# A decoder trunk on one core: the first stage on 2048 columns with unsplit float32 operands, conditioning rows in one piece, gates by themselves

## The chip, the core and the metric

One program runs on one core of a Trainium2 chip. The core has five engines with their own instruction streams: TensorE (PE: matmul, its weight loads shown as PEld), VectorE (DVE), ScalarE (ACT), GpSimd (POOL) and SyncE (SP), which here issues nearly all DMA transfers. Matmul results go to PSUM, eight banks of 512 float32 per partition; everything else lives in SBUF. The metric is the time of one execution on the device in microseconds.

## The reference

Two layers on a sequence of 256 tokens, model width 2048. A conditioning vector c gives six vectors of 2048 per layer (shift, scale and gate of two sub-layers); each comes from a matrix of 2048 x 2048 in `ada_w`. Everything is float32.

```python
mod_all = einsum('bd,lde->lbe', silu(c), ada_w) + ada_b
for i in range(2):
    sh1, sc1, g1, sh2, sc2, g2 = split(mod_all[i], 6)
    h = rms_norm(x, attn_norm_g[i]) * (1.0 + sc1) + sh1
    y = nsa_mixer(h, ...) if i == 0 else diff_mixer(h, ...)
    x = x + g1 * y
    h = rms_norm(x, mlp_norm_g[i]) * (1.0 + sc2) + sh2
    x = x + g2 * (square(relu(h @ w1)) @ w2)
```

The first mixer multiplies h by one matrix and cuts the result: q (2048 columns), kc and vc (512 each, keys and values that are compressed in blocks by two small matrices), ks and vs (512 each, selection branch), kw and vw (512 each, window branch), and 48 gates that weigh the three branches.

## The kernel before

**Layout.** Activations stand transposed: 16 tiles of 128 features (`kt`) by 256 tokens. A float32 operand is mostly split into two parts of a faster matmul type (float32r): ScalarE rounds it to a high part `wH`, VectorE subtracts to get the low part `wL` (`split`, L219), and a product takes three matmuls (`xs_mm`, `ws_mm`, L234 to L248). The normalised h is split in the same way into four activation tiles (`modulate`, L320).

**First stage (L603 to L622).** For each of the 16 `kt` it needs one column of the scale and one of the shift, each a sum over 2048 elements per partition. `ada_tile` (L160) loads such rows in halves of 1024 into `adaraw` (pool `ada`, three buffers) and VectorE multiplies by silu(c) and sums. The scale is computed so for all `kt`; the shift so for six of them; for the ten in `PEK` TensorE takes it (`ada_pe`, L173: `adapw`, a tile of 1 MB in the activation pool, and 16 float32 matmuls). Then the weights `ws` of this `kt` come in two pieces (1024 and 560 columns: kc, vc, vs, gates), are split, h of this `kt` is made, and the products for kc and vc (four PSUM tiles), vs (two) and the gates (one) are accumulated over `kt`.

**After it.** `xs_group` (L253) runs one group of 512 weight columns: four units, each two loads of 512 KB, two splits and 24 matmuls of 512 columns. The groups are ks (`k0_`), kw (`k1_`), vw (`vw_`), then four q groups, each followed by the attention of four heads whose work lies under the next group. In the two k groups each unit also does eight float32 matmuls of the compression (`hidps`, weights `cw1`). `k_block` (L700) norms and rotates the keys; its transposes wait in the list `pend` and are emitted by `pop` in the next group. After each unit `ada_step(rate)` loads rows for the later conditioning vectors, `RA` (1.1) rows per unit in k and vw groups, `RB` (1.0) in q groups; they are halves of 512 KB in the three `ada` buffers, computed on VectorE with a lowered priority.

**Queues.** All these loads are issued by SP in one order. An issue that waits for its buffer holds what stands behind it. Weight tiles `raw` have five buffers, activation tiles eight, four of which hold h. The order of instructions on each engine is set by a scheduler from the program's order, priorities and estimated times.

Of the kernel before, what the change touches and what calls it, by code (L numbers as in the profile page):

```python
# [19 lines left out]
P = 128  # L20
T = 256
# [6 lines left out]
# Points of a pair of groups where the statistics and the first group's results are taken.  # L28
# [7 lines left out]
# Tiles of the adaLN matrices taken per unit of weights, by phase.  # L36
RA, RB, RC = 1.1, 1.0, 1.6
# [5 lines left out]
# Columns of the first shift that the tensor engine takes.  # L43
PEK = [k for k in range(16) if k % 8 not in (2, 5, 7)]
# [14 lines left out]
WS_COLS = 3 * 512 + GATES  # L59
# [18 lines left out]
def emit(ctx, tc, nc, a):  # L78
# [103 lines left out]
    def ada_one(l, vec, kt):  # L182
        e = vec * KT + kt
        ac = acc_tile(l, vec)
        stt(mod[:, l, vec, kt:kt + 1], ac[:, kt, 0:1], bT[:, l, e:e + 1], ac[:, kt, 1:2], ALU.add, ALU.add)
# [32 lines left out]
    # Exact split of float32 into two float32r parts.  # L218
# [222 lines left out]
    # A norm whose first two products run on A*x before the statistics are known: the results are  # L441
    # scaled by rstd afterwards, and two further columns carry the shift through the weights.
# [156 lines left out]

    ps_c = [[mm_tile(f"psc{i}{b}") for b in range(2)] for i in range(2)]  # L600
    ps_v = [sc(f"psv{t}") for t in range(TT)]
    ps_g = sd("psg")
    for kt in range(KT):  # L603
        ada_tile(0, 1, kt)
        if kt in PEK:
            ada_pe(kt)
        else:
            ada_tile(0, 0, kt)
            ada_one(0, 0, kt)
        ada_one(0, 1, kt)  # L610
        stt(Amod[:, 0, 0, kt:kt + 1], mod[:, 0, 1, kt:kt + 1], 1.0, ag[:, 0, kt:kt + 1], ALU.add, ALU.mult)
        H, L = split(load(a["ws"][kt, :, :1024]))
        H2, L2 = split(load(a["ws"][kt, :, 1024:], WS_COLS - 1024), WS_COLS - 1024)
        modulate(h, kt, rstd, Amod[:, 0, 0, kt:kt + 1], mod[:, 0, 0, kt:kt + 1])
        f, la = kt == 0, kt == KT - 1
        for i in range(2):
            for n in range(4):
                ws_mm(ps_c[i][n // 2][:, (n % 2) * T:(n % 2 + 1) * T], h, kt, H, L, i * 512 + n * P, f and n % 2 == 0,
                      la and n % 2 == 1)
        for t in range(TT):  # L620
            xs_mm(ps_v[t], h, kt, t, H2, L2, 0, 512, f, la)
        ws_mm(ps_g[:GATES, :T], h, kt, H2, L2, 512, f, la, m=GATES)  # L622
    kcT = [actp.tile([P, GROUPS, 272], F32, tag="act", name=f"kcT{i}") for i in range(2)]
    for i in range(2):
        V.memset(kcT[i][:, :, 256:272], 0.0)
        for b in range(2):
            act(kcT[i][:, b * 2:b * 2 + 2, 0:T], ps_c[i][b].rearrange("p (g t) -> p g t", g=2))
    for t in range(TT):
        act(Vt[:, t, 0, :], ps_v[t])

    gT = wkp.tile([P, T], F32, tag="PcT", name="gT", bufs=1)
    act(gT[:48, :], ps_g[:48, :T])
    for t in range(TT):
# [399 lines left out]
```

## Time and profile before

| what | value |
|---|---|
| median of 3 runs | 2420.01 us (2419.43 to 2420.33) |
| the profiled execution: its own time, which is its span | 2418.4 us |
| PE busy | 2368.7 us, 98% |
| DVE busy | 1706.2 us, 71% |
| ACT busy | 1179.3 us, 49% |
| moved by DMA | 612.79 MB, mean 253 GB/s |
| first stage: start of the first and the last gate matmul | 31.7 and 157.9 us |
| q groups: start of the first and the last matmul | 266.0 and 420.6 us |
| mean granted TensorE clock | 0.996 |

Busy time is the sum of an engine's instruction spans; matmuls overlap in the pipeline, so their single durations are longer than their spacing. The granted clock is the share of 2.4 GHz at which TensorE was allowed to run; 0.5 is the lower of its two levels, 1.2 GHz. The DMA share is the mean busy share of the 16 DMA engines in a stretch.

### The profile page before, as it was taken

What the parts mean: (1) busy time and instruction counts of PE and PEld (TensorE: products, weight loads), DVE (VectorE), ACT (ScalarE), POOL (GpSimd) and SP (SyncE); (2) the same over time, 40 slices, a digit from 0 to 9 for tenths busy, and PEclk for the clock granted to TensorE, in tenths of its full rate; (3) what the DMA queues carried; (4) which work ended last, traced back from release to release, by engine and by line L of the source; (5) the groups of instructions that cost most, each with busy time, mean ns of one, the idle gap of its engine ahead of it and who ended that gap; (6) DMA issues with size and microseconds to landing.
All of it is one profiled execution on the core that took longest, in us unless ns stands there. A gap on an engine that the chain in (4) does not pass through costs nothing.

```text
span 2418.4 us, 44106 instructions
## 1 busy us (share of the span) xinstructions
PE 2368.7 (98%) x17683; PEld 2233.3 (92%) x17683; DVE 1706.2 (71%) x2670; ACT 1179.3 (49%) x1939; POOL 39.4 (2%) x41
## 2 busy tenths in 40 slices
PE   8889899999999999999999999999999999999999
PEld 6876677999999999999999788799999999999999
DVE  6786898999878888878897766656745445455444
ACT  3233477656434434434546655555643443443443
POOL 0000000000000000000000101100000000000000
PEclk9999999999999999999999999999999999999999
DMA  8988875787888888888986565445555555555554
GB/s 331 351 315 308 301 279 204 285 317 286 339 342 333 327 342 338 333 328 337 335 306 215 200 228 173 162 152 182 181 186 185 184 183 184 188 186 183 184 193 147
DMA packets 168973, 612.79 MB, mean 253 GB/s; under 512 B 18880, under 2 KB 20288, under 8 KB 167488
## 3 DMA queue, kind: packets, MB, share of 16 engines
q1 hardware_dynamic: 167616, 609.06, 68.6%
q8 instruction: 138, 2.26, 0.4%
q10 hardware_dynamic: 1152, 0.92, 0.2%
q14 instruction: 67, 0.55, 0.1%
HBM read 607.81 MB, written 2.10 MB: 252 GB/s over the span
## 4 chain that ended last, share of the span: by engine, by line
PE 88%; DVE 5%; DMA 3%; ACT 2%; issue 1%; POOL 1%; SPq 0%; DVEq 0%; ACTq 0%; POOLq 0%
PE m L248 19%; PE m L247 19%; PE m L246 19%; DVE wL L100 2%; DMA adaraw<-adaT 2%; DVE adaraw L103 1%; PE adps L178 1%; PE dwo L247 1%; PE dwo L246 1%; PE dwo L248 1%; PE m_z L248 1%; PE m_z L246 1%; PE m_z L247 1%; PE dq L239 1%; PE dq L238 1%
## 5 line engine op out<-in xcount | busy, mean ns | idle before, releaser
L100 DVE TENSOR_TENSOR wL<-raw,wH 128x1024 fp32r<-128x1024 f32 x760 | 920.1, 1214 | 568.3 <-ACT wH L97 565.6
L97 ACT ACTIVATE wH<-raw 128x1024 fp32r<-128x1024 f32 x760 | 796.9, 1051 | 999.2 <-PE m L247 615.4
L248 PE MATMUL m<-hd,wL 128*128 128x256 f32 x2048 | 576.6, 282 | 1.0 <-DVE wL L100 1.0
L247 PE MATMUL m<-hd,wH 128*128 128x256 f32 x2048 | 576.7, 282 | 0.0
L246 PE MATMUL m<-hd,wH 128*128 128x256 f32 x2048 | 576.4, 282 | 0.0
L247 PE MATMUL m<-hn,wH 128*128 128x256 f32 x1792 | 504.4, 282 | 0.0
L248 PE MATMUL m<-hn,wL 128*128 128x256 f32 x1792 | 503.7, 281 | 0.0
L246 PE MATMUL m<-hn,wH 128*128 128x256 f32 x1792 | 503.2, 281 | 0.0
L103 DVE SCALAR_TENSOR_TENSOR adaraw<-adaraw,cbc 128x1024 f32<-128x1024 f32 x364 | 438.3, 1220 | 21.7 <-DMA adaraw<-adaT 21.2
L248 PEld LDWEIGHTS m<-hd,wL 128*128 128x128 f32 x2048 | 387.2, 189 | 1.5 <-DVE wL L100 1.4
L247 PEld LDWEIGHTS m<-hd,wH 128*128 128x128 f32 x2048 | 386.7, 189 | 0.0
L246 PEld LDWEIGHTS m<-hd,wH 128*128 128x128 f32 x2048 | 386.2, 189 | 0.1
L246 PEld LDWEIGHTS m<-hn,wH 128*128 128x128 f32 x1792 | 338.5, 189 | 0.2 <-ACT zb L97 0.2
L248 PEld LDWEIGHTS m<-hn,wL 128*128 128x128 f32 x1792 | 338.4, 189 | 0.0
L247 PEld LDWEIGHTS m<-hn,wH 128*128 128x128 f32 x1792 | 337.7, 188 | 0.0
L248 PE MATMUL nwo<-o,wL 128*128 128x256 f32 x256 | 72.9, 285 | 2.6 <-DVE wL L100 2.6
L246 PE MATMUL nwo<-o,wH 128*128 128x256 f32 x256 | 73.4, 287 | 0.3 <-ACT wH L97 0.3
L246 PE MATMUL dwo<-od,wH 128*128 128x256 f32 x256 | 72.8, 284 | 0.0
L247 PE MATMUL nwo<-o,wH 128*128 128x256 f32 x256 | 72.4, 283 | 0.0
L248 PE MATMUL m_z<-z,wL 128*128 128x258 f32 x256 | 70.1, 283 | 2.4 <-DVE wL L100 2.4
L247 PE MATMUL dwo<-od,wH 128*128 128x256 f32 x256 | 72.1, 282 | 0.0
L248 PE MATMUL dwo<-od,wL 128*128 128x256 f32 x256 | 72.0, 281 | 0.0
(312 smaller groups left out, 3399.3 us busy)
## 6 DMA issues: line engine op xcount, KB each, us to landing
raw<-w SPq DMA_DIRECT2D x512, 512.0 KB, 4.5
adaraw<-adaT SPq DMA_DIRECT2D x364, 512.0 KB, 5.7
raw<-di SPq DMA_DIRECT2D x96, 512.0 KB, 3.6
raw<-wi SPq DMA_DIRECT2D x56, 512.0 KB, 6.3
raw<-nwo SPq DMA_DIRECT2D x32, 512.0 KB, 4.7
raw<-dwo SPq DMA_DIRECT2D x32, 512.0 KB, 3.2
adapw<-adaP SPq DMA_DIRECT2D x10, 1024.0 KB, 8.0
raw<-ws SPq DMA_DIRECT2D x16, 512.0 KB, 8.5
```

Of the source, the lines that this page charges most:

```text
L97: return S.activation(out=out, in_=in_, func=func, **kw)
L100: V.tensor_tensor(out=out, in0=in0, in1=in1, op=op)
L103: V.scalar_tensor_tensor(out, in0, scalar, in1, op0=op0, op1=op1, **kw)
L178: TE.matmul(ps[:, :P], r[:, k, :], cs[:, k:k + 1].to_broadcast([P, P]), start=(k == 0), stop=(k == KT - 1))
L238: TE.matmul(ps, xh, H[:, off:off + n], start=first, stop=False)
L239: TE.matmul(ps, xh, L[:, off:off + n], start=False, stop=False)
L246: TE.matmul(ps, H[:, off:off + m], xh, start=first, stop=False)
L247: TE.matmul(ps, H[:, off:off + m], xl, start=False, stop=False)
L248: TE.matmul(ps, L[:, off:off + m], xh, start=False, stop=last)
```

## The change

The first stage takes 2048 columns of weights (kc, vc, vs, vw) instead of 1584, in two tiles of 1024 columns, and multiplies them as they are: `modulate_full` keeps an unsplit h of the `kt` beside the split one, and the matmuls are float32. All eight PSUM tiles of the three pools hold results. Scale and shift are both done on VectorE for every `kt`, each as one instruction over 2048 elements (`ada_row`), from tiles in the activation pool. The gates are computed by `gates()` behind the kw group, from weights of their own. The vw group falls away; `pop` is called in the q groups; `RA` and `RB` become 1.3 and 1.2.

```diff
-RA, RB, RC = 1.1, 1.0, 1.6
+RA, RB, RC = 1.3, 1.2, 1.6
-WS_COLS = 3 * 512 + GATES
+WS_COLS = 4 * 512
-    def ada_pe(kt):
-        ps = sc("adps")
-        r = actp.tile([P, KT, P], F32, tag="act", name="adapw")
-        nc.sync.dma_start(r, a["adaP"][PEK.index(kt)])
-        for k in range(KT):
-            TE.matmul(ps[:, :P], r[:, k, :], cs[:, k:k + 1].to_broadcast([P, P]),
-                      start=(k == 0), stop=(k == KT - 1))
-        ts(mod[:, 0, 0, kt:kt + 1], ps[:, 0:1], bT[:, 0, kt:kt + 1], None, ALU.add)
+    def ada_row(vec, kt):
+        r = actp.tile([P, D], F32, tag="act", name="adarow")
+        nc.sync.dma_start(r.rearrange("p (j d) -> p j d", j=2),
+                          a["adaT"][0, vec * KT + kt].rearrange("j p d -> p j d"))
+        acc = acc_tile(0, vec)[:, kt, 0:1]
+        stt(r, r, 1.0, cbc, ALU.mult, ALU.mult, accum_out=acc)
+        return acc
+    def modulate_full(tiles, kt, rstd, A, sh):
+        t = sm.tile([P, T], F32, tag="nsq", name="nt0", bufs=4)
+        stt(t, xT[:, kt, :], A, rstd, ALU.mult, ALU.mult)
+        full = sm.tile([P, T], F32, tag="pp", name="h32", bufs=4)
+        act(full, t, AF.Identity, bias=sh)
+        H = tiles[kt // 4][:, 0, kt % 4, :T]
+        act(H, full)
+        tt(tiles[kt // 4][:, 1, kt % 4, :T], full, H.bitcast(F32), ALU.subtract)
+        return full
-    ps_v = [sc(f"psv{t}") for t in range(TT)]
-    ps_g = sd("psg")
+    ps_v = [[sc("psv00"), sc("psv01")], [sc("psv10"), sd("psv11")]]
     for kt in range(KT):
...
-        H, L = split(load(a["ws"][kt, :, :1024]))
-        H2, L2 = split(load(a["ws"][kt, :, 1024:], WS_COLS - 1024), WS_COLS - 1024)
-        modulate(h, kt, rstd, Amod[:, 0, 0, kt:kt + 1], mod[:, 0, 0, kt:kt + 1])
+        acc = ada_row(1, kt)
+        stt(Amod[:, 0, 0, kt:kt + 1], acc, b1[:, kt:kt + 1], ag[:, 0, kt:kt + 1], ALU.add, ALU.mult)
+        acc = ada_row(0, kt)
+        tt(mod[:, 0, 0, kt:kt + 1], acc, bT[:, 0, kt:kt + 1], ALU.add)
+        wc = load(a["ws"][kt, :, :1024])
+        wv = load(a["ws"][kt, :, 1024:])
+        full = modulate_full(h, kt, rstd, Amod[:, 0, 0, kt:kt + 1], mod[:, 0, 0, kt:kt + 1])
...
+    def gates():
+        H, L = split(load(a["wg"], KT * GATES), KT * GATES)
+        ps_g = sd("psg")
+        for kt in range(KT):
+            ws_mm(ps_g[:GATES, :T], h, kt, H, L, kt * GATES, kt == 0, kt == KT - 1, m=GATES)
...
-    ps = xs_group("vw_", lambda u: blocks[2, u], h, RA, lambda u: pop())
-    for t in range(TT):
-        act(Vt[:, t, 1, :], ps[t])
+    gates()
...
-        ps = xs_group(f"q{g}_", lambda u: blocks[3 + g, u], h, RB)
+        ps = xs_group(f"q{g}_", lambda u: blocks[2 + g, u], h, RB, lambda u: pop())
```

The program's order on SP at the start of the first stage, where `adaraw` and `adarow` are conditioning rows, `adapw` TensorE's conditioning tile and `raw<-ws` the stage's weights. Before:

```order
L168 DMA adaraw<-adaT 128x1024 x2
L176 DMA adapw<-adaP 128x2048
L228 DMA raw<-ws 128x1024
L228 DMA raw<-ws 128x560
L166 DMA adaraw<-adaT 128x1024 x2
L228 DMA raw<-ws 128x1024
L228 DMA raw<-ws 128x560
L166 DMA adaraw<-adaT 128x1024 x2
```

Now:

```order
L174 DMA adarow<-adaT 128x2x1024 x2
L221 DMA raw<-ws 128x1024 x5
L174 DMA adarow<-adaT 128x2x1024 x4
L221 DMA raw<-ws 128x1024
L174 DMA adarow<-adaT 128x2x1024 x2
L221 DMA raw<-ws 128x1024 x2
L174 DMA adarow<-adaT 128x2x1024 x2
```

The rows now come in pieces of 1 MB, two per step, and the weights of two steps and a half stand ahead of the second step's rows.

TensorE where the ks group (here `k_0`, `k_1` with the smaller numbers) ends and the kw group begins; `tps` are the transposes of the normed ks tiles `krn`, `hidps` the compression. Before, the first transposes stand here, behind the kw group's first unit:

```order
681 L240 MATMUL k_1_1713<-wH,h_199 128x512
682 L663 MATMUL hidps<-raw,bl 64x256 x8
683 L438 MATMUL tps<-co,krn 128x128 x4
684 L238 MATMUL k_0_1712<-wH,h_200 128x512
685 L238 MATMUL k_1_1713<-wH,h_200 128x512
```

Now they stand behind the ks group's last unit, ahead of the kw group's first matmul:

```order
244 L233 MATMUL k_1_762<-wH,h_202 128x512
245 L673 MATMUL hidps<-raw,bl 64x256 x8
246 L441 MATMUL tps<-co,krn 128x128 x4
247 L231 MATMUL k_0_1039<-wH,h_199 128x512
248 L231 MATMUL k_1_1040<-wH,h_199 128x512
```

The first transposes moved ahead by one unit of 24 matmuls and eight `hidps`. At the end of the kw group the gates (`psg`) now follow the last `hidps`, where the vw group began; on ScalarE the split of their weights stands between the steps of that group's norm:

```order
L95 ACTIVATE jk,kss<-k_0_1039 128x128 x4
L95 ACTIVATE jk,kss<-k_1_1040 128x128
L95 ACTIVATE krn<-k_0_1039,krs 128x128 x4
L95 ACTIVATE jk,kss<-k_1_1040 128x128
L95 ACTIVATE wH<-raw 128x768
```

Here `jk` are the sums of squares of the two token tiles, `krn` the scaled keys of the first one and `wH<-raw 128x768` the gates' weights; there is no such split in the kernel before, whose gate weights were split within the first stage.

## Rows read from the trace of the kernel before

**Rows 1.** The page: engines, and GB/s in 40 slices of 60.46 us.

```profile
PE 2368.7 (98%) x17683; PEld 2233.3 (92%) x17683; DVE 1706.2 (71%) x2670; ACT 1179.3 (49%) x1939; POOL 39.4 (2%) x41
...
GB/s 331 351 315 308 301 279 204 285 317 286 339 342 333 327 342 338 333 328 337 335 306 215 200 228 173 162 152 182 181 186 185 184 183 184 188 186 183 184 193 147
```

**Rows 2.** Windows of the first stage: length, busy times, then clock, DMA share, GB/s.

```profile
60.00:80.00 20.00, 18.02 (x131) 16.28 (x131) 15.44 (x31) 5.20 (x7) 0.00 (x0) 1.00 0.80 299
...
100.00:120.00 20.00, 18.29 (x141) 17.06 (x140) 14.64 (x31) 4.77 (x7) 0.00 (x0) 1.00 0.99 376
```

**Rows 3.** Waits of SP's queue from 0 to 150: total us, times, longest.

```profile
SPq L166 <- DVE adaraw L103: 76.9, 27, 6.9
```

**Rows 4.** DMA issues of the page: count, KB each, us to landing.

```profile
adaraw<-adaT SPq DMA_DIRECT2D x364, 512.0 KB, 5.7
...
raw<-wi SPq DMA_DIRECT2D x56, 512.0 KB, 6.3
...
adapw<-adaP SPq DMA_DIRECT2D x10, 1024.0 KB, 8.0
raw<-ws SPq DMA_DIRECT2D x16, 512.0 KB, 8.5
raw<-cw SPq DMA_DIRECT2D x16, 512.0 KB, 7.1
raw<-ws SPq DMA_DIRECT2D x16, 280.0 KB, 8.7
```

**Rows 5.** The chain that ended last, its first piece: start, us.

```profile
0.74 3.63 DMA smallT<-smallT
```

**Rows 6.** Groups by line and shape, 0 to 180: busy us, mean ns.

```profile
L100 DVE TENSOR_TENSOR wL<-raw,wH 128x1024 fp32r<-128x1024 f32 x22 | 26.9, 1223 | 18.2 <-ACT wH L97 18.2
...
L100 DVE TENSOR_TENSOR wL<-raw,wH 128x560 fp32r<-128x560 f32 x16 | 11.8, 739 | 4.8 <-ACT wH L97 4.8
...
L97 ACT ACTIVATE h<-nt,mod 128x256 fp32r<-128x256 f32 x16 | 8.1, 508 | 41.9 <-DVE mod L107 34.3 <-DVE mod L103 5.4 <-DVE nt L103 2.2
```

**Rows 7.** Timeline of PE: start, us; x32 and x16 count two passes a float32 matmul.

```profile
11.68 7.07 PE L339 MATMUL nps<-nsq,ones 128*128 128x256 f32 x32
...
168.07 0.50 PE L238 MATMUL k<-wH,h 128*128 128x512 f32 x1
...
173.84 3.67 PE L663 MATMUL hidps<-raw,bl 128*64 128x256 f32 x16
```

**Rows 8.** Tiles k and vw: ns min/median/max, first and last start.

```profile
L238 PE MATMUL k<-wH,h x64: 387/396/504, 158.1 to 233.7; 128*128 128x512 f32 x64
...
L238 PE MATMUL vw<-wH,h x32: 387/395/502, 238.1 to 265.3; 128*128 128x512 f32 x32
```

**Rows 9.** Timeline of PE at four waits; in brackets the idle time before.

```profile
83.03 0.74 PE L246 MATMUL psc<-h,wH 128*128 128x256 f32 x4 [3.05 <-ACT h L97]
...
103.80 0.39 PE L246 MATMUL psc<-h,wH 128*128 128x256 f32 x1 [0.85 <-ACT h L97]
...
207.72 0.50 PE L239 MATMUL k<-wL,h 128*128 128x512 f32 x1 [1.07 <-DVE wL L100]
...
278.91 0.79 PE L238 MATMUL q<-wH,h 128*128 128x512 f32 x2 [4.07 <-ACT wH L97]
```

**Rows 10.** Windows of 5 us behind two of these waits.

```profile
85.00:90.00 5.00, 5.00 (x26) 4.66 (x25) 2.34 (x7) 1.62 (x2) 0.00 (x0) 0.67 1.01 410
280.00:285.00 5.00, 4.83 (x16) 3.86 (x17) 4.64 (x7) 2.12 (x2) 0.00 (x0) 0.71 0.97 372
```

**Rows 11.** Timeline: the ks group's last matmul, the sum that ends its norm.

```profile
192.25 0.39 PE L240 MATMUL k<-wH,h 128*128 128x512 f32 x1
...
200.63 0.62 DVE L100 TENSOR_TENSOR krn<-krn,t 128x512 f32<-128x512 f32 x1
```

**Rows 12.** Windows of the q groups.

```profile
300.00:340.00 40.00, 38.58 (x203) 30.10 (x202) 38.09 (x106) 32.14 (x98) 1.69 (x2) 1.00 0.81 285
340.00:380.00 40.00, 40.00 (x212) 31.35 (x211) 36.26 (x103) 31.31 (x96) 1.58 (x2) 1.00 0.60 210
```

More of the change, by code (lines that the diff above doesn't have):

```diff
@@ L42 @@
 NEARLY = 2
-PEK = [k for k in range(16) if k % 8 not in (2, 5, 7)]
 ACT_SET = "natural_log_exp_and_others"
@@ L598, in emit @@
     gate = cst.tile([P, TT, 48], F32, name="gate")
+    b1 = cst.tile([P, KT], F32, name="b1")
+    ts(b1, bT[:, 0, KT:2 * KT], 1.0, None, ALU.add)
     ps_c = [[mm_tile(f"psc{i}{b}") for b in range(2)] for i in range(2)]
-    ps_v = [sc(f"psv{t}") for t in range(TT)]
-    ps_g = sd("psg")
+    ps_v = [[sc("psv00"), sc("psv01")], [sc("psv10"), sd("psv11")]]
     for kt in range(KT):
[L604 to L611, printed above, removed]
-        H, L = split(load(a["ws"][kt, :, :1024]))
-        H2, L2 = split(load(a["ws"][kt, :, 1024:], WS_COLS - 1024), WS_COLS - 1024)
-        modulate(h, kt, rstd, Amod[:, 0, 0, kt:kt + 1], mod[:, 0, 0, kt:kt + 1])
+        acc = ada_row(1, kt)
[5 more added lines that the diff above has]
+        full = modulate_full(h, kt, rstd, Amod[:, 0, 0, kt:kt + 1], mod[:, 0, 0, kt:kt + 1])
         f, la = kt == 0, kt == KT - 1
@@ L617, in emit @@
             for n in range(4):
-                ws_mm(ps_c[i][n // 2][:, (n % 2) * T:(n % 2 + 1) * T], h, kt, H, L, i * 512 + n * P, f and n % 2 == 0,
-                      la and n % 2 == 1)
-        for t in range(TT):
-            xs_mm(ps_v[t], h, kt, t, H2, L2, 0, 512, f, la)
-        ws_mm(ps_g[:GATES, :T], h, kt, H2, L2, 512, f, la, m=GATES)
+                TE.matmul(ps_c[i][n // 2][:, (n % 2) * T:(n % 2 + 1) * T], wc[:, i * 512 + n * P:i * 512 + (n + 1) * P],
+                          full, start=f and n % 2 == 0, stop=la and n % 2 == 1)
+        for i in range(2):
+            for t in range(TT):
+                TE.matmul(ps_v[i][t], full[:, t * P:(t + 1) * P], wv[:, i * 512:(i + 1) * 512], start=f, stop=la)
     kcT = [actp.tile([P, GROUPS, 272], F32, tag="act", name=f"kcT{i}") for i in range(2)]
@@ L626, in emit @@
         for b in range(2):
[L627 to L633, printed above, removed]
-        ps = sd("gps")
-        TE.transpose(ps[:, :48], gT[:48, t * P:(t + 1) * P], ident[:48, :48])
-        act(gate[:, t, :], ps[:, :48], AF.Exp, scale=-1.0)
-    ts(gate, gate, 1.0, None, ALU.add)
-    V.reciprocal(gate, gate)
+            src = ps_c[i][b].rearrange("p (g t) -> p g t", g=2)
+            if b:
+                V.tensor_copy(kcT[i][:, 2:4, 0:T], src)
+            else:
+                act(kcT[i][:, 0:2, 0:T], src)
+    for i in range(2):
+        for t in range(TT):
+            act(Vt[:, t, i, :], ps_v[i][t])
+    def gates():
[3 more added lines that the diff above has]
+            ws_mm(ps_g[:GATES, :T], h, kt, H, L, kt * GATES, kt == 0, kt == KT - 1, m=GATES)
+        gT = wkp.tile([P, T], F32, tag="PcT", name="gT", bufs=1)
+        act(gT[:48, :], ps_g[:48, :T])
+        for t in range(TT):
+            ps = sd("gps")
+            TE.transpose(ps[:, :48], gT[:48, t * P:(t + 1) * P], ident[:48, :48])
+            act(gate[:, t, :], ps[:, :48], AF.Exp, scale=-1.0)
+        ts(gate, gate, 1.0, None, ALU.add)
+        V.reciprocal(gate, gate)
     nc.sync.dma_start(posi, a["posT"])
@@ L991 @@
     ins["adaT"] = c_(ada_w.transpose(0, 2, 1).reshape(DEPTH, NVEC, P, 2, D // 2).transpose(0, 1, 3, 2, 4))
-    ins["adaP"] = c_(ada_w[0][:, :D].reshape(KT, P, KT, P).transpose(2, 1, 0, 3)[PEK])
     wi = nsa_w_in[0]
```

10 lines of the change are left out of this document (3 added, 7 removed).

## Prediction

> **What bounds the kernel now.** I went from the whole to the stage that the diff edits. TensorE is busy 98% of the span [rows 1], so time that leaves its queue, and any wait of it, counts one to one wherever nothing else is late. The exception is the opening: the page's line of moved bytes gives 331 and 351 GB/s for the first two slices of 60 us [rows 1], and the windows there show queues that are sometimes full (share 0.99, 376 GB/s) and sometimes not (0.80, 299 GB/s), while TensorE is busy 18 of 20 us in both [rows 2]. Look at how VectorE is far from full too (about 15 of 20). So the first stage ends neither with TensorE nor with VectorE, but with the loads. Why the queue runs dry is in the waits of SP: 76.9 us in 27 waits on VectorE's multiply-and-sum over `adaraw` [rows 3]. SP issues in order; `adaraw` has three buffers of 512 KB, and everything behind a blocked `adaraw` issue, the weights too, starts late.
>
> After it, the k, v and q groups run on TensorE at its own pace: 24 matmuls from 168.07 to 173.84, then eight of `cw1` in 3.7 us [rows 7]; their loads come in time until the turn from `vw` to the first q group.
>
> **The change, part by part.** *First stage, loads.* Before, it loads 44 `adaraw` of 512 KB, 10 `adapw` of 1024 KB and 16 pairs of `ws` tiles of 512 and 280 KB [rows 4]: 46.5 MB, with 2.1 MB of x ahead. After: 64 half rows of 512 KB (as 32 wide ones) and 32 `ws` tiles of 512 KB, 50.3 MB. That is 3.8 MB more. But the buffers differ: the wide rows rotate through the four activation buffers that the four h tiles leave free (4 MB, two whole steps), the weights through five. A step moves 3.15 MB. While one lands, the next is already issued: the first row's buffer is free 2.3 us after landing, the weights' when TensorE has used them, and that is 11 us or so ahead of need. So I take the queue as full throughout. A full queue gave 376 GB/s over 20 us [rows 2] and 410 over 5 us [rows 10]; I take 385, nearer the longer window. 52.4 / 0.385 = 136 us, plus 4 us of start (the first small load lands at 4.4 [rows 5]): the last weights land at 140.
>
> Here a page speaks of the same quantity. The Trainium skill, "HBM Reference", section "Specifications (TRN2)", gives a core about 358 GB/s as its share of the memory and about 425 when it streams alone. By 358 the loads end at 150 and the kernel at about 2411; by 425 TensorE would become the stage's limit and the kernel would end near 2393. The rows lie between the two, above the share.
>
> *First stage, compute.* A conditioning row of 2048 costs one instruction: 1223 ns for 1024 columns against 739 for 560 is 1.04 ns a column, so 1223 + 1068 = 2.29 us [rows 6]. Two of them and five small ones make some 6.5 us of VectorE a step. TensorE: a float32 matmul of 256 columns takes 7.07 / 16 = 0.44 us [rows 7] and one of 512 twice that, so a step is 8 x 0.44 + 4 x 0.88 = 7.0 us. (Three split ones of 256 are 3 x 0.12, so unsplit operands cost TensorE more; the splits on ScalarE and VectorE, and the ten columns that TensorE summed, are saved.) Loads need 3.15 / 0.385 = 8.2 us a step, more than either. That cover is thin: 1.2 us on TensorE. The last shift row lands 1.05 MB before the end, at 137.3; 2.3 us of VectorE, ScalarE's 0.5 us [rows 6] and the small ones between them bring TensorE's last step to 141, its end to 148. The first k group starts then, against 158.1 now [rows 8]: **-10 us** (376 GB/s: -7; 410: TensorE becomes the limit soon after, at most -17). Filling every PSUM bank is hidden: the banks of kc and vc close 3.5 us before the last matmul. For the splits of the first k tile, which now stand behind those copies on ScalarE and VectorE, I add **+1** (0 to 2).
>
> *The `vw` group goes.* 96 matmuls of 512 columns at 5.77 / 24 = 0.24 us [rows 7]: **-23 us** of TensorE, out of the stretch whose first matmuls start at 238.1 and last at 265.3 [rows 8]. Its small companions (transposes, the end of the value compression) move under the first q group and cost the same.
>
> *The gates on their own.* 48 matmuls of 256 columns at half of 0.24: **+6 us** on TensorE, which is no longer waiting there for loads; in the first stage they were covered.
>
> *Two new waits.* The order puts the transposes of the first k tile directly behind the last `cw1` matmuls of its group; before, a whole unit of the next group stood between. The chain that they wait for (squares, power on GpSimd, scaling, two rope products, sum) ended at 201.25, 8.7 us past the group's last matmul [rows 11]. Without the two weight splits that ScalarE did in it I estimate 7.1 us; 3.7 us of `cw1` cover half. And behind the second k group stand the gates, whose split of `wg` ScalarE and VectorE do only after the same chain: again about 3.4 us. After gaps of 3.05 and 4.07 us [rows 9] the granted clock was 0.67 and 0.71 in the next 5 us [rows 10], part of it at 1.2 GHz: 1.6 us lost each time. Two times 5: **+10 us** (0 if the scheduler's order hides them after all, 13 if the whole 8.7 stays).
>
> *The wait that may go.* The 4.07 us at 278.91, the first q group waiting for its weights, with 1.5 us of low clock behind it. `vw` and q together ask 2.2 MB for each 5.8 us, 380 GB/s, the queue's limit. Now the stretch from gates to the end of that group loads 9.8 MB in 31 us or more: **-6 us** (0 if VectorE holds the row buffers as before).
>
> *Rates 1.3 and 1.2.* Ten rows instead of eight in the k groups: 27 MB in 80 us, 340 GB/s, covered. In the q groups 19 instead of 16, two of the three in groups 1 to 3. There VectorE is busy 38.1 and 36.3 of 40 us with TensorE at 38.6 and 40.0 [rows 12]; 5 us more in 126 leave little air: **+2** (0 to 5).
>
> Sum: -10 + 1 - 23 + 6 + 10 - 6 + 2 = -20 us. The profiled execution took 2418.4; the median of the runs is 2420.0, 1.6 above it. So **2400 us**. A run of this kernel differs from the next by well under 0.1%; I count as no change what lies within 0.2%, 4.8 us.
>
> **The rivals.** *More gain*: no stall behind the k groups, or a queue at 400 GB/s. For it: around the same chain TensorE waited only 1.07 us before [rows 9]. Sum -30, **2390**. Chance 0.17.
>
> *Less gain*: the q wait stays and VectorE's rows slow the q groups by 5 us instead of 2: -20 + 6 + 3 = -11, **2409**. For it: VectorE's share there. Against: its rows come last in priority. Chance 0.14.
>
> *The queue doesn't get faster.* It keeps its average of 341 GB/s [rows 1]: 52.4 / 0.341 + 4 = 158, stage end 166, +8 instead of -10: **2418**, no change. For it: SP's in-order waits could move from `adaraw` to the weight tiles, which TensorE now holds until used. Against: five of them and 11 us of lead. Chance 0.10.
>
> *Slower: TensorE at half clock in the first stage.* Each of the 16 steps ends in a pause for the next row. If the clock falls there, a step takes 14 us instead of 8.2 and is bound by TensorE. It decides from 20 / 5.8 = 3.4 such steps on; all 16 give +93, **2493**. Against: pauses of 0.85 us, such as that before 103.80 [rows 9], left the clock at 1.00 in that window [rows 2]; 1.2 us is nearer to them than to 3.05. The Trainium skill, "TensorE: Matmul & The Clock Gate", section "Loop structure matters more than you think", warns of exactly this shape, a load wait ahead of every burst of matmuls; the rows bear it out for the long pauses alone. With other losses, a queue at 300 GB/s among them, chance 0.09.
>
> **How the numbers follow.** The forecast has 0.50, with a range of its own of 2394 to 2406. Adding more and less gain makes 0.81, from 2386 (the stage at its best, half of the new waits hidden) to 2413 (376 GB/s, the waits at 13, the q wait kept). Faster 0.81, same 0.10, slower 0.09.
>
> **What would show it.** The first k matmul near 148 and windows of 370 GB/s or more with SP's waits on the rows gone; TensorE idle 3 to 4 us before the k transposes and before the gates, and a granted clock below 1 behind each; no 4 us gap in the first q group; the q groups at about 42 us each. It is wrong if the windows of the first stage show 340 GB/s, if the clock there stays at half, or if the distance from the last q group to the end changes by more than 3 us, since nothing in it is edited.

## The result and the profile after

The changed kernel takes **2395.26 us** (median of 4 runs, 2393.43 to 2397.17), against 2419.72 us for the kernel before on the same chip (4 runs, 2417.71 to 2420.33): a ratio of 0.9897, 95% interval 0.9883 to 0.9912. 2400 was forecast, with 2386 to 2413 as the range. The profiled execution, from which all rows below are, has a span of 2393.7 us (2418.4 before).

The page's rows that answer to [rows 1]: TensorE is busy the same share of the span as before, and the first two slices move 376 and 414 GB/s instead of 331 and 351.

```profile
PE 2352.3 (98%) x17171; PEld 2189.6 (91%) x17171; DVE 1688.2 (71%) x2594; ACT 1150.2 (48%) x1914; POOL 41.2 (2%) x41
...
GB/s 376 414 327 302 300 261 262 284 305 313 328 340 337 339 332 322 341 330 333 328 295 205 208 198 176 156 152 185 180 188 184 180 189 185 184 186 184 185 194 149
```

I cut both traces at the first matmul of each kind of work, and read a window for each stretch. After: the first stage, the k groups with the gates, the q groups, nwo (the first mixer's output matrix, under which the last attention work runs), the first MLP pair (two groups of the first MLP matrix that are computed together, tile `m_z`), and the four last together (columns: length, busy time of PE, PEld, DVE, ACT, POOL with the number of instructions, then clock, DMA share, GB/s). The last cut is the first matmul behind that pair; the expectations below call it the second MLP matrix, but it still belongs to the first one.

```profile
23.43:143.45 120.02, 114.39 (x384) 73.85 (x385) 92.45 (x139) 18.55 (x38) 0.00 (x0) 0.98 1.01 402
143.45:240.09 96.64, 88.44 (x385) 61.96 (x384) 69.23 (x118) 33.48 (x77) 6.78 (x5) 0.95 0.80 296
240.09:387.25 147.16, 146.18 (x747) 113.98 (x745) 137.92 (x358) 103.47 (x299) 6.04 (x6) 1.00 0.80 279
387.25:506.02 118.77, 116.75 (x918) 111.94 (x917) 107.56 (x234) 70.74 (x161) 2.01 (x2) 1.00 0.81 285
506.02:561.74 55.72, 50.06 (x395) 49.10 (x393) 54.19 (x93) 30.69 (x54) 0.00 (x0) 0.97 0.81 281
143.45:561.74 418.29, 401.44 (x2438) 336.98 (x2436) 368.90 (x800) 238.38 (x590) 14.83 (x13) 0.98 0.81 285
```

The same cuts in the trace before lie at 25.41, 158.05, 265.96, 420.81, 536.99 and 588.20. Put beside what the prediction gave for each (its terms summed by place):

| stretch | before, us | after, us | change | predicted | TensorE idle before / after |
|---|---|---|---|---|---|
| start to the first k matmul | 158.05 | 143.45 | -14.6 | -9 | 17.0 / 5.6 in the stage |
| k groups, vw or gates | 107.9 | 96.6 | -11.3 | -7 | 3.0 / 8.2 |
| q groups | 154.9 | 147.2 | -7.7 | -4 | 6.1 / 1.0 |
| nwo | 116.2 | 118.8 | +2.6 | 0 | 4.0 / 2.0 |
| first MLP pair | 51.2 | 55.7 | +4.5 | 0 | 2.5 / 5.7 |
| the rest of the span | 1830.2 | 1832.0 | +1.8 | 0 | |
| sum | | | -24.7 | -20 | |

TensorE's own work in the first stage hardly moved (115.7 us busy before, 114.4 now); what went there is idle time (2.0 of the 14.6 us lie ahead of the stage's first matmul, at 23.43 instead of 25.41). SP's 76.9 us of waits for VectorE to free a row's buffer [rows 3] are down to some 9. SP now waits for weight buffers that TensorE holds, and the queue is full all the same. From 0 to 150, total us, times, longest:

```profile
SPq L221 <- PE psc L618: 59.0, 16, 10.5
SPq L221 <- PE psv L622: 27.6, 13, 3.0
SPq L174 <- DVE mod L98: 5.4, 3, 2.7
```

The k groups show a stall at the turn from the first to the second. PE there, start and length, in brackets the idle time before and what ended it; the last two rows are the gates:

```profile
181.07 1.94 PE L673 MATMUL hidps<-raw,bl 128*64 128x256 f32 x8 [1.21 <-DMA raw<-cw]
184.09 0.63 PE L441 MATMUL tps<-co,krn 128*128 128x128 f32 x4 [1.08 <-DVE krn L98]
186.26 1.22 PE L231 MATMUL k<-wH,h 128*128 128x512 f32 x2 [1.54 <-ACT wH L95]
188.80 0.79 PE L232 MATMUL k<-wL,h 128*128 128x512 f32 x1 [1.31 <-DVE wL L98]
...
231.72 0.32 PE L239 MATMUL psg<-h,wH 128*48 128x256 f32 x1 [0.95 <-ACT wH L95]
233.12 0.32 PE L241 MATMUL psg<-h,wL 128*48 128x256 f32 x1 [0.97 <-DVE wL L98]
```

At and behind the first four waits, 5.1 us together, the granted clock falls, part of the time to 1.2 GHz, as it did behind those of [rows 9, 10]; the windows from 185 and from 190 show 0.59 and 0.73:

```profile
185.00:190.00 5.00, 2.42 (x5) 1.51 (x6) 4.70 (x10) 2.88 (x6) 0.00 (x0) 0.59 0.91 353
190.00:195.00 5.00, 5.00 (x18) 3.96 (x17) 5.00 (x7) 2.12 (x2) 0.00 (x0) 0.73 0.89 288
```

SP's queue ahead of that place (start, time in issue, xcount) shows why weights were late. This unit takes two rows, that is four half rows, for three buffers. The fourth waits until 175.61 for VectorE to let one go, and the weights behind it, half of `cw1` and those of the next k unit, go out only then:

```profile
164.25 3.33 SPq L164 DMA_DIRECT2D adaraw<-adaT  x3
167.68 0.38 SPq L221 DMA_DIRECT2D raw<-cw  x1
175.61 0.33 SPq L164 DMA_DIRECT2D adaraw<-adaT  x1
176.03 0.38 SPq L221 DMA_DIRECT2D raw<-cw  x1
176.51 0.86 SPq L221 DMA_DIRECT2D raw<-wi  x2
```

And in the first MLP pair TensorE waits for the second half of a split that VectorE takes late:

```profile
514.94 0.75 PE L241 MATMUL m_z<-z,wL 128*128 128x258 f32 x4 [2.45 <-DVE wL L98]
529.46 0.75 PE L241 MATMUL m_z<-z,wL 128*128 128x258 f32 x4 [2.74 <-DVE wL L98]
```

### The profile page after: what moved, and what is told of

It is laid out like the page before. It is cut to its first block, busy times and chain, and to the rows that moved or that the text cites. A ratio compares the mean times of both kernels' runs of the same rounds, so it can differ in the third digit from the quotient of the medians.

```text
span 2393.7 us, 42873 instructions
## 1 busy us (share of the span) xinstructions
PE 2352.3 (98%) x17171; PEld 2189.6 (91%) x17171; DVE 1688.2 (71%) x2594; ACT 1150.2 (48%) x1914; POOL 41.2 (2%) x41
## 4 chain that ended last, share of the span: by engine, by line
PE 86%; DVE 6%; DMA 4%; ACT 2%; issue 1%; POOL 1%; SPq 0%; DVEq 0%; ACTq 0%; POOLq 0%
PE m L241 19%; PE m L239 19%; PE m L240 19%; DMA adaraw<-adaT 2%; DMA adarow<-adaT 2%; DVE wL L98 2%; PE dwo L240 1%; PE dwo L239 1%; PE dwo L241 1%; PE psc L618 1%; DVE adaraw L101 1%; PE m_z L241 1%; PE m_z L240 1%; PE m_z L239 1%; DVE adarow L101 1%
## 5 line engine op out<-in xcount | busy, mean ns | idle before, releaser
L98 DVE TENSOR_TENSOR wL<-raw,wH 128x1024 fp32r<-128x1024 f32 x721 | 880.1, 1223 | 544.8 <-ACT wH L95 541.3
L95 ACT ACTIVATE wH<-raw 128x1024 fp32r<-128x1024 f32 x721 | 762.7, 1059 | 947.5 <-PE m L240 684.7
L101 DVE SCALAR_TENSOR_TENSOR adaraw<-adaraw,cbc 128x1024 f32<-128x1024 f32 x320 | 385.7, 1218 | 16.2 <-DMA adaraw<-adaT 15.9
L101 DVE SCALAR_TENSOR_TENSOR adarow<-adarow,cbc 128x2048 f32<-128x2048 f32 x32 | 73.2, 2287 | 14.1 <-DMA adarow<-adaT 14.1
L618 PEld LDWEIGHTS psc<-h,raw 128*128 128x128 f32 x256 | 49.5, 197 | 26.4 <-ACT h L95 17.9
L239 PE MATMUL nwo<-o,wH 128*128 128x256 f32 x256 | 73.3, 286 | 0.0
L239 PE MATMUL m_z<-z,wH 128*128 128x258 f32 x256 | 72.9, 286 | 0.0
L239 PE MATMUL dwo<-od,wH 128*128 128x256 f32 x256 | 72.9, 285 | 0.0
```

The source lines that it names most:

```text
L95: return S.activation(out=out, in_=in_, func=func, **kw)
L98: V.tensor_tensor(out=out, in0=in0, in1=in1, op=op)
L101: V.scalar_tensor_tensor(out, in0, scalar, in1, op0=op0, op1=op1, **kw)
L239: TE.matmul(ps, H[:, off:off + m], xh, start=first, stop=False)
L618: TE.matmul(ps_c[i][n // 2][:, (n % 2) * T:(n % 2 + 1) * T], wc[:, i * 512 + n * P:i * 512 + (n + 1) * P], full, start=f and n % 2 == 0, s ...
```

## The experiments

Twelve kernels, in four sets; each set was timed beside the kernel before, so ratios are to it (0.9897 for the changed kernel, whose own runs were not in these sets). "k to m" is the stretch from the first k matmul to the first matmul behind the MLP pair, 430.2 us before and 418.3 after.

Each stretch is read from one profiled execution per kernel, and it differs between kernels that don't differ in it. In the seven kernels below that leave the first stage and what stands ahead of it as changed, the first k matmul comes between 141.3 and 145.1. In three that edit nothing behind that stage (without two products, narrow rows, split operands) k to m takes 414.9, 419.3 and 422.0 us, and its first part, to the first q matmul, 93.0, 97.8 and 99.2. A difference of that size says nothing about its edit.

### Loads or TensorE in the first stage: a step without two products

```
-        for i in range(2):
+        for i in range(2 if kt in (0, KT - 1) else 1):
             for t in range(TT):
                 TE.matmul(ps_v[i][t], ...)
```

> The changed kernel without the second pair of value products in 14 of the 16 steps of the first stage (its result is left out, the loads stay): TensorE's step falls from 7.0 to 5.2 us. Theory (loads and TensorE are within a few per cent of each other, the loads at 400 to 416 GB/s need 7.6 to 7.9 us a step): the first k matmul moves from 143.5 to no earlier than 138. Rival 1 (TensorE alone bounds the stage): the steps shorten to some 5.5 us, the first k matmul comes near 120. Rival 2 (VectorE's 6.5 us chain of two rows bounds it): near 136, with the queue less than full.

Measured: first k matmul at 140.87, 2.6 us earlier than with all products; 2390.2 us, one run. Windows of this run, the whole stage first:

```profile
22.78:140.87 118.09, 96.38 (x328) 65.61 (x329) 92.22 (x140) 18.47 (x38) 0.00 (x0) 0.94 1.02 410
...
40.00:60.00 20.00, 14.17 (x52) 9.27 (x51) 15.07 (x24) 2.77 (x6) 0.00 (x0) 1.00 1.03 414
...
100.00:120.00 20.00, 14.76 (x47) 9.41 (x45) 14.71 (x23) 2.03 (x5) 0.00 (x0) 0.91 1.03 413
```

TensorE now idles 22 of 118 us and the stage hardly shortens, while the queue is full. The loads are the limit of the changed first stage, and both rivals fall. What TensorE's two products cost on top is 2.6 us at most: 140.87 is hardly outside the 141.3 to 145.1 of kernels that have them.

### The row buffers undone

```
     def ada_row(vec, kt):
-        r = actp.tile([P, D], F32, tag="act", name="adarow")
...                                one load of 1 MB, one multiply-and-sum go
+        ada_tile(0, vec, kt)
+        ac = acc_tile(0, vec)
+        tt(ac[:, kt, 0:1], ac[:, kt, 0:1], ac[:, kt, 1:2], ALU.add)
...
```

> The changed kernel with the two first conditioning vectors as half rows of 512 KB through the three buffers of the kernel before, and all else as changed. Theory of the prediction (the gain of the first stage is the queue, which in-order SP starved behind three buffers): windows of the first stage fall to 330 to 370 GB/s, the first k matmul comes at 152 to 162 instead of 143.5, the kernel at 2404 to 2412. Rival (TensorE's unsplit operands and VectorE without the weight splits are the gain, the row buffers don't matter): first k matmul within 3 us of 143.5.

Measured: first k matmul at 181.91; 2438.27 us (2 runs), ratio 1.0072 (1.0052 to 1.0092). SP's waits from 0 to 150 (total us, times, longest), and the stage as one window:

```profile
SPq L164 <- DVE adaraw L101: 77.8, 25, 5.8
```

```profile
23.00:181.91 158.91, 126.09 (x384) 80.96 (x385) 99.98 (x224) 17.81 (x37) 0.00 (x0) 0.90 0.87 308
```

The first k matmul comes 38.5 us later than in the changed kernel, and the stage, the rate and the time (2404 to 2412 expected) are all worse than the far end that I gave. With half rows through three buffers the same wait as in [rows 3] is back, and the queue moves 308 GB/s. The mechanism holds; the rival falls. Three things go together here, the size of a load, the bytes of buffer (1.5 MB instead of 4) and the number of instructions on VectorE; no run separates them.

### The unsplit operands undone

```
-        wc = load(a["ws"][kt, :, :1024])
-        wv = load(a["ws"][kt, :, 1024:])
+        H, L = split(load(a["ws"][kt, :, :1024]))
+        H2, L2 = split(load(a["ws"][kt, :, 1024:]))
...                                the same for h; three matmuls a product again
```

> The changed kernel with the 2048 columns of the first stage split into two float32r parts again (two splits of 1.0 us on ScalarE and 1.22 us on VectorE a step more, three matmuls of a quarter of the time each instead of one). VectorE gets 2 x 2.37 + 2 x 1.22 + 5 small ones, 8.5 us a step, against 7.6 us of loads; TensorE falls from 7.0 to 5.7 us. Theory (unsplit operands are what lets VectorE take both vectors): a step takes 8.5 us or more, the first k matmul comes at 155 to 165, the kernel at 2407 to 2417. Rival (the splits hide): first k matmul at 143 to 147, since the weights' buffers come free earlier.

Measured: first k matmul at 154.04; 2410.78 us (3 runs), ratio 0.9963 (0.9944 to 0.9982). The stage, and SP's waits in it:

```profile
25.25:154.04 128.79, 106.96 (x576) 91.39 (x577) 123.26 (x162) 40.32 (x51) 0.00 (x0) 0.91 0.98 380
```

```profile
SPq L221 <- DVE wL L98: 52.8, 18, 6.5
```

VectorE is busy 123.3 of 128.8 us, and the weights' buffers wait for it: 10.6 us lost. The kernel's time is as expected; the first k matmul comes 1 us before the range of the theory, with 8.05 us a step instead of 8.5.

### Wide rows alone, in the kernel before

```
-        ada_tile(0, 1, kt)
+        ada_row(1, kt)
         if kt in PEK:
             ada_pe(kt)
         else:
-            ada_tile(0, 0, kt)
...
+            ada_row(0, kt)
...
```

(`ada_row` as in the changed kernel, with the bias added at its end)

> The kernel before with one part of the change: the conditioning rows that VectorE takes in the first stage (16 of the scale, 6 of the shift) come as wide rows of 1 MB into the activation buffers, with one multiply-and-sum each; the ten columns on TensorE, the split weights and the vw group stay. Theory (three row buffers of 512 KB starved the queue; in the changed kernel with narrow rows the first k matmul came at 181.9 instead of 143.5): SP's waits on the rows go, the windows reach 390 GB/s or more, the first k matmul moves from 158 to 135 to 145 (46.5 + 2.1 MB), the kernel to about 2400. Rival (the unsplit operands are needed too, since TensorE and the splits hold the weights' buffers): first k matmul at 152 or later, the kernel at 2413 or more.

Measured: **slower than before**: 2441.0 us, ratio 1.0081 (1.0060 to 1.0102), first k matmul at 176.09 instead of 158.05. My theory, that the queue depth alone was worth the gain, falls; the result lies on the rival's side (152 or later, 2413 or more), and far out. The waits of SP, VectorE and ScalarE in the stage:

```profile
SPq L236 <- DVE wL L100: 66.3, 15, 8.9
DVE wL L100 <- ACT wH L97: 33.0, 17, 4.9
ACT h L97 <- DVE mod L107: 38.6, 9, 7.0
```

The row buffers hardly hold SP up any longer; now it waits 66.3 us for weight buffers that the second half of a split, on VectorE, has not let go. VectorE is not full (105 of the stage's 150 us); it waits in turn for ScalarE's half, and ScalarE, in order, for the shift from TensorE's columns (34.3 us of such waits stood there before [rows 6]). Wide rows and the 1 MB `adapw` of these columns share four buffers here. Windows swing between a full and a starved queue:

```profile
120.00:140.00 20.00, 18.88 (x143) 17.26 (x141) 12.84 (x21) 6.50 (x9) 0.00 (x0) 1.00 0.67 244
140.00:160.00 20.00, 12.84 (x81) 11.64 (x82) 12.78 (x20) 3.97 (x5) 0.00 (x0) 0.83 0.99 390
```

This run is not a clean test of the rows. The built order also moved the sines' work on VectorE into the stage, to 61 to 78 us (150 to 163 before), where TensorE then pauses 6.87 us; how much of the loss is due to that is open.

So unsplit weights with half rows (narrow rows, above) and wide rows with split weights and `adapw` both end slower than before, and the changed kernel with split weights (the run before this one) keeps some 10 of the 25 us. Of the changes to the first stage, wide rows and unsplit weights are both needed for the whole gain. That `adapw` is what spoils this run, and that its removal is the third condition, is argued from the shared buffers; no run takes it alone out.

### The stall of the k groups: transposes and gates moved

```
             cmp_part(i, hp, u)
-            pop()
+            if i and u == 1:
+                gates()
+            if u:
+                pop()
...
-    gates()
...
-        ps = xs_group(..., h, RB, lambda u: pop())
+        ps = xs_group(..., h, RB, lambda u: pop() if u else None)
```

> The changed kernel with the transposes of both k tiles taken one unit of weights later, and with the gates' projection inside the second k group instead of behind it. Theory (the two new waits cost about what their gaps and the low clock behind them show: 1.21 + 1.08 + 1.54 + 1.31 us around the first transposes with clocks of 0.59 and 0.73 behind them, 0.95 + 0.97 us at the gates with 0.87 and 0.79): first k matmul to first q matmul falls from 96.6 us to 87 to 90, the kernel to about 2388. Rival 1 (the time is given back where VectorE is full, in the q groups and the first MLP pair): the stretch shortens the same, the stretch from the first q matmul to the second MLP matrix grows by as much, the kernel stays at 2395. Rival 2 (the waits only move on to the next instruction): the stretch stays at 96.

Measured: 2394.79 us (4 runs), ratio 0.9884 (0.9868 to 0.9901), not told apart from 0.9897. First k to first q matmul 92.9 us (96.6), k to m 417.2. The transposes stand elsewhere, but at the turn TensorE still waits 1.12 us for `cw1`, then 3.35 us for the split of the late weights, then 1.32: 5.8 us against 5.1. In the changed kernel the norm's chain ends one of the waits (1.08 us, `krn`), but without it TensorE stands as long for the weights; so the chain, to which I had put this stall, was not what held it. The gates' two waits of 0.95 and 0.97 us are gone. That the 3.7 us up to the first q matmul come from there is not shown: without any edit here the run without two products took 93.0.

### The sines worked out early

```
     for kt in range(KT):
+        if kt == 1:
+            trig()
...
-    trig()
```

(with the load of the positions at the program's start)

> The changed kernel with the sines and cosines of the positions worked out during the second step of the first stage instead of between the first stage and the second unit of the first k group. Theory (the 3.17 us gap before that unit is ScalarE's, with its two table loads and the chain on VectorE between the splits): the gap falls below 1 us, the kernel to 2392 or 2393. Rival (it is the weight tile that lands late, since TensorE holds the buffers): the gap stays above 2.5 us and the kernel at 2395. A loss is possible if the 6 us of VectorE delay a step of the first stage: first k matmul later than 143.5 by up to 3.

Measured: 2401.16 us, ratio 0.9911 (0.9896 to 0.9926); first k matmul at 150.02. The gap of 3.17 us that this was to remove was a misreading of mine. Eight float32 matmuls, recorded as sixteen passes from 149.83 on, fill it in the trace of the changed kernel:

```profile
149.83 3.67 PE L673 MATMUL hidps<-raw,bl 128*64 128x256 f32 x16
153.43 0.50 PE L231 MATMUL k<-wH,h 128*128 128x512 f32 x1
```

What the run shows is the loss it named as possible, at twice the size: 6.6 us. In its second step VectorE stood 4.01 us in front of a table's operand still in flight, with the conditioning rows in order behind it, and TensorE waited 5.41 us.

### The rates undone

```
-RA, RB, RC = 1.3, 1.2, 1.6
+RA, RB, RC = 1.1, 1.0, 1.6
```

> The changed kernel with the rates of the kernel before, 1.1 and 1.0 instead of 1.3 and 1.2. Theory of the prediction (the rates cost 2 us by filling VectorE in the q groups): the kernel falls to 2393, the q stretch from 147.2 to 145. Rival 1 (rows that are not done in the q groups come due in the next stretch, where VectorE is full): the q stretch falls, the stretch from the first nwo matmul to the second MLP matrix grows by 5 us or more, the kernel goes to 2398 or more. Rival 2: no difference within 1 us.

Measured: 2397.94 us, ratio 0.9900 (0.9885 to 0.9915): no difference. Inside, much moved: first k to first q matmul 87.6 us instead of 96.6, with 3.4 us of waits left at the turn, none at the gates, and the clock at 1.00; q groups 151.9 (147.2), nwo 120.9 (118.8), first MLP pair 58.9 (55.7). The theory of the prediction falls; of the first rival, nwo and the pair grew by 5.3 us as it said, but the q stretch did not shrink. What the k groups gave was lost further on, which made me think that VectorE as a whole set the pace of k to m.

### VectorE relieved, in two ways

```
-                stt(r, r, 1.0, cbc[:, j * 1024:(j + 1) * 1024], ...)
+                stt(r[:, :512], r[:, :512], 1.0, cbc[:, j * 1024:j * 1024 + 512], ...)
```

> The changed kernel with the multiply-and-sum over the later conditioning rows taken on half of their columns (the other half of these sums is left out; the loads stay): 112 rows of 1.22 us between the first k matmul and the second MLP matrix become some 0.68 us, 60 us less of VectorE there. Theory A (VectorE, busy 369 of 418 us and fed late by its own order, sets the length of the stretch, so a wait that is taken away comes back further on): the stretch falls from 418 us to 400 to 405, where TensorE's own 395 us of matmuls end it, and the waits on VectorE in the k groups, in nwo and in the first MLP pair go together; the kernel goes to about 2380. Theory B (the new waits are each local: the norm's chain, late weight tiles): the stretch stays within 4 us of 418, the kernel at 2391 or more.

This kernel leaves out half of each of these sums. Measured: 2398.16 us, one run; k to m **425.2**, longer, with VectorE busy 316 us in it instead of 369:

```profile
141.58:566.80 425.22, 402.83 (x2438) 337.99 (x2436) 316.24 (x804) 238.91 (x590) 14.80 (x13) 0.98 0.78 283
```

```
-PMA = ((0, 1), (0, 2), (1, 1))
+PMA = tuple((t, b) for t in range(2) for b in range(3))
```

> The changed kernel with all six scalings of a head's probabilities on ScalarE instead of three on each engine: 48 instructions of 0.27 us, 13 us with what lies between them, leave VectorE between the first q group and nwo, some 17 us come to ScalarE, which is busy 28 to 31 of 37 us. Theory A (VectorE sets the stretch): the first k matmul to the second MLP matrix falls from 418 to 408 to 413, the kernel to about 2388. Theory B (local waits): no change within 2 us. Rival C (ScalarE becomes the limit in the q groups): the q stretch grows from 147 to over 150, the kernel slower than 2395.

Measured: 2402.41 us, ratio 0.9923 (0.9906 to 0.9939); k to m 426.6. The q stretch fell to 143.8 us, yet nwo rose to 133.9: its end waits for splits on ScalarE now:

```profile
488.54 0.39 PE L239 MATMUL nwo<-o,wH 128*128 128x256 f32 x1 [3.01 <-ACT wH L95]
...
496.56 0.58 PE L239 MATMUL nwo<-o,wH 128*128 128x256 f32 x1 [1.75 <-ACT wH L95]
```

Theory A falls: 53 us less of VectorE brought nothing. C, in the form in which I put it, falls too, since the q stretch did not grow, though the kernel is slower as it said. What is left as an explanation, and not shown by these two runs, is the order in which ScalarE and VectorE take splits among their other work. That order is fixed when the kernel is built, and it came out anew with each edit.

### Fewer rows in the k groups, more in the q groups

```
-RA, RB, RC = 1.3, 1.2, 1.6
+RA, RB, RC = 1.1, 1.4, 1.6
```

> The changed kernel with 1.1 rows a unit in the k groups instead of 1.3, and 1.4 in the q groups instead of 1.2, nothing else. Theory (the stall around the first k transposes is in good part SP, stuck 7.5 us on a third row of one unit with the weights of the next unit behind it; with the rates of before the k groups and gates took 87.6 us instead of 96.6, but the rows left over were missed before the first MLP pair, where 13.5 us of idle TensorE stand instead of 7.8): first k to first q matmul 87 to 90 us, the q groups 147 to 150, nwo and the first MLP pair together 172 to 176, the kernel at 2386 to 2391. Rival (what a wait gives up here comes back in the order of the splits further on): first k matmul to second MLP matrix stays at 416 to 420, the kernel at 2395.

Measured: 2390.38 us (4 runs), ratio 0.9876 (0.9857 to 0.9894). First k to first q matmul 87.6 us as expected, nwo and the pair 175.3 too; the q groups take 152.8 and not 147 to 150; k to m 415.6. The profiled executions of the changed kernel and of this one lie 6.0 us apart, 2.1 of them ahead of the first k matmul, where nothing was edited. The k groups with the gates, as one window:

```profile
141.30:228.92 87.62, 84.18 (x385) 59.25 (x384) 62.41 (x106) 32.02 (x75) 6.40 (x5) 1.00 0.81 296
```

TensorE idles 3.4 us in it instead of 8.2, and the clock is 1.00 instead of 0.95: half of the 9 us are waits, the other half what the low clock behind them had cost. SP's queue at the turn has two half rows a unit, and the weights leave at 168.81 instead of 176.51 (the whole stretch stands 2.1 us earlier):

```profile
163.75 4.96 SPq L221 DMA_DIRECT2D raw<-cw  x2
168.81 1.63 SPq L221 DMA_DIRECT2D raw<-wi  x2
170.49 3.32 SPq L164 DMA_DIRECT2D adaraw<-adaT  x2
173.90 4.18 SPq L221 DMA_DIRECT2D raw<-cw  x2
```

> As the run with 1.1 and 1.4 rows a unit, with the later transposes and the gates inside the second k group as well. Theory (the two causes of the stalls, rows ahead of weights and the norm's chain, add up): first k to first q matmul 85 to 88 us, the kernel 1 to 3 us under the run with the rates alone. Rival: the order of the splits in the q groups, nwo and the first MLP pair gives it back, no difference within 2 us, or slower, as when the moved transposes alone took 3.7 us off up to the first q matmul and gave 2.3 back up to the second MLP matrix.

Measured, with the moved transposes and gates on top: 2394.97 us, ratio 0.9889 (0.9866 to 0.9912); first k to first q matmul 87.5, the same as without. That the 9 us belong to the rate in the k groups is the firmest reading of these runs: the four kernels with 1.1 rows take 87.5 to 87.6 us, the eight with 1.3 rows 92.9 to 99.2. With 1.1 rows the built order had put the transposes a unit later by itself, so a low rate with early transposes was not run. The rival is right: k to m is 421.1, with one wait of 7.49 us for a split at nwo's end. (What the moved transposes had given back behind the first q matmul is 2.7 us by the windows, not the 2.3 of the expectation.)

### One place of that order

```
-RA, RB, RC = 1.3, 1.2, 1.6
+RA, RB, RC = 1.1, 1.4, 1.6
...
-            for kt in range(12):
-                tn.scale(kt)
+            with tc.high_priority(offset=-60):
+                for kt in range(12):
+                    tn.scale(kt)
```

> The run with 1.1 and 1.4 rows a unit, with the twelve scalings of x ahead of the first MLP pair put behind at lower priority, so that on ScalarE one split of weights now stands between the sixth and the seventh of them instead of behind all twelve. There TensorE stood 3.81 us waiting for that split and 2.29 us for its second half on VectorE. Theory (these waits come from the order on ScalarE and VectorE, not from their load): of these 6.1 us about 3 go, the first nwo to the second MLP matrix takes 171 to 174 us instead of 175.3, the kernel 2386 to 2389, under both kernels. Rival (the wait comes up again at the next split or in the pair): first k matmul to second MLP matrix stays at 415 to 417, the kernel at 2390 or 2391.

Measured: **2388.07 us** (4 runs, 2386.70 to 2392.05), ratio 0.9871 (0.9851 to 0.9891). At nwo's end, c_rates first:

```profile
480.08 0.39 PE L239 MATMUL nwo<-o,wH 128*128 128x256 f32 x1 [3.81 <-ACT wH L95]
483.12 0.58 PE L241 MATMUL nwo<-o,wL 128*128 128x256 f32 x1 [2.29 <-DVE wL L98]
```

and with the scalings behind:

```profile
481.15 0.39 PE L239 MATMUL nwo<-o,wH 128*128 128x256 f32 x1 [1.35 <-ACT wH L95]
482.41 0.50 PE L241 MATMUL nwo<-o,wL 128*128 128x256 f32 x1 [0.52 <-DVE wL L98]
```

6.1 us became 1.9: these waits came from the order on ScalarE, where the split now stands between the scalings and not behind all of them. nwo fell by 4.0 us, the pair rose from 52.1 to 54.1, and k to m is 413.2, 2.4 us shorter and the shortest of all. That the kernel gains by it is not shown: nwo and the pair together (173.3 us) are only 2.0 us below the run without this edit, and in the changed kernel and the three that edit nothing behind the first stage they range from 174.2 to 175.8. It has the lowest median of the study, but its interval overlaps that of the run with the rates alone and that of the changed kernel, and none of them were run side by side.

## Why the prediction was right, step by step

**The first stage** was right in cause, too small in size: -14.6 instead of -9. The mis-sized term is the queue's rate. I took 385 GB/s between two rows; the stage's window shows 402, and 410 with less work for TensorE. That the loads bind and not TensorE was right (first run above), and so was a thin cover of TensorE by the loads: it idles 5.6 us in the stage. The Trainium skill, "HBM Reference", section "Specifications (TRN2)", gives about 425 GB/s for a core that streams alone and 358 as its share; the 410 measured over that whole stage lies near the first and above the share. The row of VectorE was exact (2.29 us predicted, 2287 ns over 32):

```profile
L101 DVE SCALAR_TENSOR_TENSOR adarow<-adarow,cbc 128x2048 f32<-128x2048 f32 x32 | 73.2, 2287 | 14.1 <-DMA adarow<-adaT 14.1
```

The +1 for late splits of the first k tile did not come: the k matmuls start as the last value product ends. The rival "the queue doesn't get faster" named its mechanism rightly, SP's waits did move to the weight tiles (86.6 us), but with five buffers the queue stayed full. What the step did not see is that the wide rows gave the whole gain only with the unsplit weights.

**Behind the first stage** the sum was right within 1 us, -11.9 for -11 from the first k matmul to the end of the pair, and that is in part luck: its terms missed in both directions, as follows.

**vw, gates and the new waits** summed to -7, and -11.3 was measured. vw's stretch of 27.9 us is gone; 23 are its own matmuls, and the rest is mostly its small companions, which moved on as foretold (the stretch held 123 matmuls, 96 of them vw's; in turn nwo has 29 more now, attention work from the q groups). The gates take 8.4 us, 5.7 where nothing waits (6 predicted), and the k groups 8.2 longer: 10.9 for the 10 that I gave the two waits. The size held by luck, the cause did not: I put it to the norm's chain and its transposes, and gave the rate of 1.3 in the k groups nothing. Of the 3 to 4 us of idle time foretold before the transposes and before the gates, 1.1 and 1.9 us came. With 1.1 rows a unit 9 of these 10.9 us go; about 2 are left, and the waits there are for splits of weights, not for the chain. "27 MB in 80 us, covered" was true of the mean, and false at the turn, where the four half rows of one unit block in-order SP for 7.5 us with the weights behind.

**The first q group's wait** went, as predicted: no wait over 0.6 us is left there, against 4.07 in [rows 9]. The q stretch shrank by 7.7 instead of 4; part of that is attention work that now runs in the nwo stretch (918 matmuls there instead of 889). The "about 42 us each" that I named for a q group was a wrong reading: four took 154.9 us before, 38.7 each, and take 36.8 now. The +2 for the rate in the q groups does not show in the changed kernel, whose q stretch idles 1.0 us. No run moves that rate alone from there. Two kernels with 1.1 rows in the k groups differ in it, 1.0 against 1.4 rows a unit in the q groups, the stretch of each:

```profile
229.75:381.67 151.92, 150.92 (x775) 117.81 (x773) 136.38 (x355) 107.79 (x315) 6.04 (x6) 1.00 0.72 253
228.92:381.67 152.75, 148.48 (x757) 115.93 (x756) 143.41 (x369) 106.60 (x311) 6.05 (x6) 1.00 0.82 283
```

With more rows TensorE idles 4.3 us there instead of 1.0, the way of the forecast. That the first of them is 4.7 us longer than the changed kernel's 147.2 says nothing of the rates: it holds 28 more matmuls, 775 instead of 747, and nwo about as many fewer.

**The sign that I named as making it wrong did come**: the distance from the last q group to the end grew by 8.9 us, with nothing in it edited. 2.6 of it is the nwo stretch with the moved attention work, 4.5 the first MLP pair, where 3.2 us more of waits for splits and a clock of 0.97 stand, and 1.8 the unedited rest. That VectorE's load is not the cause is shown: with 53 us less of it k to m was no shorter (one run). That the order on the two splitting engines is the cause is shown for one pair of waits (6.1 us became 1.9), and argued for the rest. Why the built order falls well in one kernel and badly in the next was not settled.

**The rivals.** The result lies midway between the forecast and "more gain" (2390), whose queue of 400 GB/s came and whose "no stall" did not. That rival was priced too high: by the forecast's own sum 400 GB/s ends the loads at 135 instead of 140, worth 5 us and not 10, and 2395 is what came. The slower rival, half clock from a pause in each step, was put to the test by the run without two products: pauses of 1.4 to 3.0 us in most steps, and a granted clock of 0.91 to 1.00 in windows of 20 us. The Trainium skill, "TensorE: Matmul & The Clock Gate", section "Loop structure matters more than you think", warns of such a loop; with pauses of this length the clock stayed far from half, and with one of 6.87 us (wide rows alone) the window of 20 us around it shows 0.76.

## What to carry to other kernels

Where one queue issues everything in order, count its loads per unit at the worst place, not on average: a buffer that a slow consumer holds there delays every load behind it. Parts of a change can each lose alone and win together, if one part frees the engine that the other part's buffers wait for; so test the parts before crediting one. Where two engines prepare operands for a third, look at the order of that preparation before believing that an engine's load is the limit. And read a stretch in a few kernels that don't differ in it before crediting an edit with what it gained there.

## What the runs showed of the hardware

One core's loads of 0.5 and 1 MB held 413 and 414 GB/s in windows of 20 us and 410 over 118 us (the run without two products); the 20 us shown of before had 376 [rows 2]. TensorE idle for 18% of that stage (22 of 118 us, in pauses of up to 3.0 us) kept a mean granted clock of 0.94. In the k groups of the changed kernel, where 5.1 us of waits fell within 9 us, the windows of 5 us from 185 and 190 show 0.59 and 0.73, between the two levels of 1.2 and 2.4 GHz; with 1.1 rows a unit, 3.4 us of waits over the same stretch left the clock at 1.00. A float32 row of 2048 columns times a vector, with its sum, took VectorE 2287 ns.
